# The first 400 tokens of a hybrid encoder block: loaded twice, or transposed on TensorE

## The chip, the cores and the metric

The kernel runs on one core of one Trainium2 chip. Its engines are TensorE (PE, whose weight loads the profile lists as PEld), VectorE (DVE), ScalarE (ACT), GpSimd (POOL) and SyncE (SP), whose queue issues all DMAs here. The metric is device time in microseconds (us) of one execution. The profile's times count from the first instruction of a profiled execution; "L810" is line 810 of the kernel before.

## What is computed

One layer of an encoder with two groups of heads. A sequence of 16 meta tokens, 256 prompt tokens and 2048 sample tokens (2320 in all, 1024 wide, float32) is normalised, projected to 2816 columns, handled by windowed attention and by a convolution, and projected back:

```python
def rmsnorm(x, w):
    y = x * lax.rsqrt(jnp.mean(x * x, axis=-1, keepdims=True) + NORM_EPS)
    return y * w

def hybrid_layer(z, norm_w, w_in, ..., w_out):
    h = rmsnorm(z, norm_w)
    proj = jnp.einsum('bld,de->ble', h, w_in)
    q, k, v, g_att, c_val, c_glu, g_conv = jnp.split(proj, SPLIT_IDX, axis=-1)
    ...
    att = windowed_gqa(q, k, v, sink) * jax.nn.silu(g_att)
    cnv = conformer_conv(c_val, c_glu, conv_w, conv_b, ln_w, ln_b) * jax.nn.silu(g_conv)
    mixed = jnp.concatenate([att, cnv], axis=-1)
    return z + jnp.einsum('ble,ed->bld', mixed, w_out)
```

The change touches only how `h` and the first weights reach TensorE at the start of the kernel.

## The kernel before

**Groups and units.** The tokens are cut into six groups: group 0 has 400 tokens (16 meta tokens and three blocks of 128), the others have 384. The columns of `w_in` are cut into units of 256. For the projections the tokens must lie along the free dimension and the 1024 inputs along the partitions, in eight steps `d` of 128. So the host passes `z` twice: by rows (`z`) and transposed (`zt`).

**Exact products.** A value is split into a high part (a cast to the fp32r type, by ScalarE) and a low part (the difference, by DVE or POOL). One exact product is three matmuls: high by high, high by low, low by high (`PASSES`). One sum of a projection (`proj_et`, L810) is 8 steps times 3, 24 matmuls into one bank of PSUM. A unit takes two sums for each group (its columns 0 to 127 and 128 to 255). The first items are unit 0 and unit 1 on group 0, then on group 1, then on group 2.

**Preparing a group.** `stats(i)` loads 128 rows of `z` (16 for i = 0) into a tile `xn`, squares them in place on ScalarE with a sum along the row (L679), and POOL makes `rstd` of the sum (L128, L129). `Prep.load` loads four pieces of `zt` of the group (L696); `first` lays `rstd` out along the free dimension by transposing its broadcast on TensorE (L708, into `bc`); `scale` multiplies `zt` by the norm weight and `bc` on DVE (L724); `split` makes high and low parts (L741 on ScalarE, L750 on DVE and POOL). Group g needs the stats 3g+1 to 3g+3, group 0 the stats 0 to 3.

**Weights.** `weights(k)` gives a load of four pieces (L776) and a split of each (L785 on ScalarE, L786 on DVE or POOL).

**Order.** Instructions are traced in program order and then arranged on each engine by a scheduler that simulates the engines' times. `tc.keep_in_program_order(op)` pins an instruction behind the one traced just before it on the same engine. It fixes the order only, and adds no wait for that one's result. An engine takes its instructions in this order, and waits at one whose inputs are not there.

**The opening (L1040 to L1063).** SP issues stats 0 to 3, `vecs` (norm weight and other small vectors), two pieces of `zt`, the four of unit 0, two more of `zt`, the convolution's weights. DVE derives `nsnk` and `kscale` from `vecs` (L1050, L1051). Then come the rests of stats 0 to 3, `first`, and piece by piece scaling, split of x and split of the weight. Stats 4 to 6 and the weights of unit 1 are loaded after that, and group 1's `zt` at the first item (`at_item_start`).

**Tiles.** Tag "us" (pool `cp`, four buffers) holds `xn` 0 to 5, then unit 1's raw weights, later the convolution's inputs. Tag "xn" (pool `sp`, two buffers) holds later `xn`. Tag "y" (pool `yp`, four buffers) holds the convolution's outputs. PSUM has four tags, "a" to "d", of two banks each; the sums use "a" and "b" in turn.

Of the kernel before, what the change touches and what calls it, by code (L numbers as in the profile page):

```python
# [11 lines left out]
F32 = mybir.dt.float32  # L12
F32R = mybir.dt.float32r
BF16 = mybir.dt.bfloat16
AF = mybir.ActivationFunctionType
ALU = mybir.AluOpType
AX = mybir.AxisListType

P = 128
D = 1024  # L20
ND = D // P
NM = 16
# [17 lines left out]
YW = 1280  # L40
UWID = 1197
# [23 lines left out]
GROUPS = [(0, 400)] + [(400 + 384 * i, 384) for i in range(5)]  # L65
# [14 lines left out]
def hymba_kernel(  # L80
# [11 lines left out]
    nc = tc.nc  # L92
# [3 lines left out]
    psum = ctx.enter_context(tc.tile_pool(name="psum", bufs=2, space=bass.MemoryType.PSUM))  # L96
# [11 lines left out]
    ident = const.tile([P, P], F32, name="ident")  # L108
    make_identity(nc, ident)
    vec = const.tile([P, 30], F32, name="vec")  # L110
    nw = vec[:, 0:8]
# [12 lines left out]
    rstd = const.tile([P, NB + 1], F32, name="rstd")  # L124
# [59 lines left out]
    yp = y_pools.enter_context(tc.tile_pool(name="yp", bufs=4, side="left"))  # L184
    wr = wr_pools.enter_context(tc.tile_pool(name="wr", bufs=1, side="right"))
    sp = right_pools.enter_context(tc.tile_pool(name="sp", bufs=2, side="right"))
    cp = right_pools.enter_context(tc.tile_pool(name="cp", bufs=4, side="right"))
# [475 lines left out]
        left_pools.close()  # L663

    if True:
        def stats(i):
            rows = NM if i == 0 else P
            r0 = 0 if i == 0 else NM + P * (i - 1)
            if i < 6:
                xn = cp.tile([P, UWID], F32, tag="us", name=f"xn{i}")[:, :D]  # L670
            else:
                xn = sp.tile([P, D], F32, tag="xn", name=f"xn{i}")
            dma = nc.sync.dma_start(xn[:rows], z[r0 : r0 + rows, :])
            if i >= PIN_X:
                tc.keep_in_program_order(dma)

            def rest():
                ssq = sp.tile([P, 1], F32, tag="ssq", name=f"ssq{i}", bufs=4)
                nc.scalar.activation(xn[:rows], xn[:rows], AF.Square, accum_out=ssq[:rows])  # L679
                rsqrt(rstd[:rows, i : i + 1], ssq[:rows], 1.0 / D, EPS)  # L680

            return rest

        xg = {}
# [70 lines left out]
        def weights(k):  # L755

            key = keys[k]
            raw = {}

            def load(eng):  # L760
                pool = wl if k % 2 else wr
                ws = pool.tile([P, ND, 2, UW], F32R, tag="ws", name=f"ws{key[0]}_{key[1]}")
                wsplit[key] = ws
                if key[0] == 1 and key[1] >= CACHE:
                    for q in range(4):
                        part = ws[:, 2 * q : 2 * q + 2].rearrange("p d a n -> p (d a n)")
                        eng.dma_start(part.bitcast(F32), wd[key[1], q])
                    return
                for q in range(4):
                    if k == 1:  # L770
                        if q % 2 == 0:
                            pair = cp.tile([P, UWID], F32, tag="us", name=f"wraw{k}_{q}")
                        raw[q] = pair[:, 512 * (q % 2) : 512 * (q % 2) + 512].rearrange("p (a n) -> p a n", n=UW)
                    else:
                        raw[q] = sp.tile([P, 2, UW], F32, tag="wraw", name=f"wraw{k}_{q}", bufs=4)
                    dma = eng.dma_start(raw[q], w_in[key[1], :, 2 * q : 2 * q + 2, :])  # L776
                    if PIN_W <= k < 4:
                        tc.keep_in_program_order(dma)

            def split(q, eng):  # L780
                if key[0] == 1 and key[1] >= CACHE:
                    return
                ws = wsplit[key]
                hi, lo = ws[:, 2 * q : 2 * q + 2, 0, :], ws[:, 2 * q : 2 * q + 2, 1, :]
                nc.scalar.copy(hi, raw[q])  # L785
                eng.tensor_tensor(lo, raw[q], hi, op=ALU.subtract)  # L786
                if key[0] == 0 and key[1] >= CACHE:
                    part = ws[:, 2 * q : 2 * q + 2].rearrange("p d a n -> p (d a n)")
                    later(1, lambda: nc.sync.dma_start(wd[key[1], q], part.bitcast(F32)))

            return load, split

        pj_n = [0]
# [42 lines left out]
        us = {}  # L836
# [200 lines left out]
        for k in range(2, len(keys)):  # L1037
            loads.setdefault(last_at[keys[k - 2]], []).append(k)

        preps = [Prep(g, False) for g in range(6)]  # L1040
        w01 = [weights(k) for k in range(2)]
        r = {i: stats(i) for i in (0, 1, 2, 3)}
        nc.sync.dma_start(vec[:, 0:28], vecs)
        preps[0].load(0)
        preps[0].load(1)
        w01[0][0](nc.sync)
        preps[0].load(2)
        preps[0].load(3)
        nc.sync.dma_start(cw, conv_w)
        nc.vector.tensor_scalar(nsnk, snk, -1.0, None, op0=ALU.mult)  # L1050
        nc.vector.scalar_tensor_tensor(kscale, vec[:, 20:21], -(HD ** -0.5), vec[:, 21:22], op0=ALU.mult, op1=ALU.mult)  # L1051
        for i in (0, 1, 2, 3):
            r[i]()
        preps[0].first()
        preps[0].alloc()
        preps[0].scale(0)
        for q in range(4):
            if q < 3:
                preps[0].scale(q + 1)
            preps[0].split(q)  # L1060
            w01[0][1](q, nc.gpsimd if q % 2 else nc.vector)
        r = {i: stats(i) for i in (4, 5, 6)}
        w01[1][0](nc.sync)  # L1063

        def at_item_start(i, c, u, g):
            if (c, u, g) == (1, ORDER[0], CHUNKS[1][1]):
                nc.sync.dma_start(km.bitcast(F32), kmd)
                for r0 in range(0, P, NM):
                    nc.sync.dma_start(vm[r0 : r0 + NM].rearrange("p a e -> p (a e)").bitcast(F32), vmd)
            if i == 0:  # L1070
                r[4]()
                r[5]()
                for q in range(4):
                    preps[1].load(q)
                    w01[1][1](q, nc.gpsimd if q % 2 else nc.vector)
                r[6]()
            if i == 1:
                later(1, preps[1].first)
                later(1, preps[1].alloc)
                later(1, lambda: preps[1].scale(0))  # L1080
                for q in range(4):
                    if q < 3:
                        later(1, lambda q=q: preps[1].scale(q + 1))
                    later(1, lambda q=q: preps[1].split(q))
                for k in range(7, 10):
                    later(1, lambda k=k: later(1, stats(k)))
                for q in range(4):
                    later(2, lambda q=q: preps[2].load(q))
            if i == I2:
                later(1, preps[2].first)  # L1090
                later(1, preps[2].alloc)
                later(1, lambda: preps[2].scale(0))
                for q in range(4):
                    if q < 3:
                        later(1, lambda q=q: preps[2].scale(q + 1))
                    later(1, lambda q=q: preps[2].split(q))
# [128 lines left out]
```

## Time and profile before

| | us |
|---|---|
| median of three runs | 963.74 (962.9 to 964.27) |
| the profiled execution's own time | 963.51 |
| its span, from first to last instruction | 961.7 |

In the profile each engine's busy time is given with its share of the span. A line of the timeline reads: start, duration of the group, engine, source line, operation, output tile <- input tiles, shapes, count; in brackets the idle time just before it and what ended it. A line of the view of waits reads: engine and tile that waited, what it waited for, then the total, the number and the longest. A line of a stage reads: the stretch and its length, then for PE, PEld, DVE, ACT and POOL the busy time and number of instructions, the granted TensorE clock (1.00 is full), the DMA share and GB/s. A line of a group of instructions reads: shapes and count, then busy time in us and mean of one in ns, then idle time before.

### The profile page before, as it was taken

The numbers are of one execution on the slowest core, as the hardware profiler recorded it, in microseconds if no ns is written. First come the engines' busy times: TensorE is split into PE (matmuls) and PEld (weight loads), VectorE is DVE, ScalarE is ACT, GpSimd is POOL, SyncE is SP. The second block draws the span as 40 slices with busy tenths as digits, with TensorE's granted clock in tenths as the row PEclk, the third lists the DMA queues.
The fourth block names the chain that finished last, engine by engine and source line by source line (L and its number), as shares of the span: only waits on it lengthen the run. The fifth ranks groups of instructions, "written<-read, shape, count | busy, mean of one in ns | idle before, by whom it ended". The sixth has DMA issues, their size and how long they took to land. (4 is left out here: it accounts for less than half of the span.)

```text
span 961.7 us, 16263 instructions
## 1 busy us (share of the span) xinstructions
PE 941.8 (98%) x5721; PEld 884.9 (92%) x5721; DVE 751.5 (78%) x1261; ACT 428.9 (45%) x1163; POOL 343.4 (36%) x542
## 2 busy tenths in 40 slices
PE   5999999999999999999999989999999999999998
PEld 4999999999999999999999989988888888888886
DVE  4659999988977789999996655767776777777773
ACT  7621112353458651011112456556665666656661
POOL 5600000264569300000002455655444554545442
PEclk9999999999999999999999999999999999999999
DMA  9653345784646597233334765964554355544411
GB/s 335 223 191 114 132 172 181 257 288 171 222 151 190 182 321 268 88 121 130 137 137 140 225 240 179 404 200 157 162 174 134 126 174 152 178 127 137 132 56 66
DMA packets 122528, 172.50 MB, mean 179 GB/s; under 512 B 10032, under 2 KB 84928, under 8 KB 122448
## 3 DMA queue, kind: packets, MB, share of 16 engines
q1 hardware_dynamic: 122448, 171.47, 52.7%
q8 instruction: 45, 0.74, 0.3%
q14 instruction: 35, 0.29, 0.1%
HBM read 108.74 MB, written 62.70 MB: 178 GB/s over the span
## 5 line engine op out<-in xcount | busy, mean ns | idle before, releaser
L810 PE MATMUL pj<-xh,ws 128*128 128x384 f32 (+1 forms) x1536 | 398.0, 340 | 2.8 <-ACT xh L741 2.8
L893 DVE SCALAR_TENSOR_TENSOR y<-us,cw,y 128x1167 f32<-128x1167 f32 x240 | 329.0, 1428 | 0.3
L810 PEld LDWEIGHTS pj<-xh,ws 128*128 128x128 f32 x1536 | 281.5, 189 | 3.1 <-ACT xh L741 3.1
L810 PE MATMUL pj<-xl,ws 128*128 128x384 f32 (+1 forms) x768 | 261.6, 341 | 0.0
L578 PE MATMUL y<-wo,rest 128*128 128x512 f32 x648 | 173.3, 404 | 0.0
L826 PE MATMUL pj<-ws,xh 128*128 128x256 f32 (+1 forms) x880 | 166.3, 285 | 1.4 <-DVE kn L982 1.0
L810 PEld LDWEIGHTS pj<-xl,ws 128*128 128x128 f32 x768 | 144.9, 189 | 0.4 <-DVE xl L750 0.3
L826 PEld LDWEIGHTS pj<-ws,xh 128*128 128x128 f32 (+1 forms) x880 | 137.5, 188 | 2.8 <-ACT sqq L927 1.2
L578 PEld LDWEIGHTS y<-wo,rest 128*128 128x128 f32 x648 | 115.2, 189 | 20.4
L826 PE MATMUL pj<-ws,xl 128*128 128x256 f32 (+1 forms) x440 | 124.8, 284 | 0.0
L416 ACT ACTIVATE sb<-sb,nm 128x304 f32<-128x304 f32 (+4 forms) x144 | 77.1, 535 | 61.9 <-DVE nm L404 59.3
L474 DVE TENSOR_TENSOR ptiles<-pT,ptiles 128x512 fp32r<-128x512 f32 x100 | 68.5, 686 | 31.4 <-ACT ptiles L473 30.7
L918 ACT ACTIVATE go<-pj 128x384 f32<-128x384 f32 x48 | 23.5, 490 | 153.5 <-PE pj L810 145.5
L404 DVE CUSTOM_DVE_ANT_0 sb<-S,bias,vec 128x304 f32<-128x304 f32 (+4 forms) x144 | 73.6, 511 | 14.6 <-PE S L349 11.8
L128 POOL TENSOR_SCALAR ssk<-ssk 128x2 f32<-128x2 f32 x18 | 9.3, 516 | 208.7 <-ACT sqk L932 206.8
L826 PEld LDWEIGHTS pj<-ws,xl 128*128 128x128 f32 (+1 forms) x440 | 83.0, 189 | 0.3
L439 POOL TENSOR_SCALAR sb<-sb,es 128x304 f32<-128x304 f32 (+4 forms) x144 | 71.9, 516 | 3.6
L473 ACT CAST ptiles<-pT 128x512 fp32r<-128x512 f32 x100 | 58.1, 581 | 32.0 <-PE pT L462 31.3
L497 PE MATMUL O<-ptiles,v 128*128 128x512 f32 x200 | 64.6, 402 | 0.0
L349 PEld LDWEIGHTS S<-kw,q 128*128 128x128 f32 x288 | 53.0, 188 | 12.6 <-issue 1.7
L349 PE MATMUL S<-kw,q 128*128 128x304 f32 (+4 forms) x288 | 61.9, 297 | 1.5 <-DVE q L372 1.5
L128 POOL TENSOR_SCALAR ssq<-ssq 128x4 f32<-128x4 f32 (+2 forms) x55 | 25.8, 470 | 101.7 <-ACT xn L679 78.0
(118 smaller groups left out, 1258.1 us busy)
## 6 DMA issues: line engine op xcount, KB each, us to landing
wd<-ws SPq DMA_DIRECT2D x36, 512.0 KB, 5.5
ws<-wd SPq DMA_DIRECT2D x36, 512.0 KB, 6.0
wraw<-in_w_in SPq DMA_DIRECT2D x52, 256.0 KB, 5.8
xn<-in_z SPq DMA_DIRECT2D x18, 512.0 KB, 5.9
gd<-go SPq DMA_DIRECT2D x48, 192.0 KB, 2.1
yo<-in_z SPq DMA_DIRECT2D x36, 256.0 KB, 3.4
out_y<-yo SPq DMA_DIRECT2D x36, 256.0 KB, 2.2
kw<-kd SPq DMA_DIRECT2D x16, 512.0 KB, 5.2
```

Of the source, the lines that this page charges most:

```text
L128: nc.gpsimd.tensor_scalar(src, src, scale, eps, op0=ALU.mult, op1=ALU.add)
L349: r = f(*a, **k)
L404: nc.vector.tensor_tensor_reduce(out=sb[:, n, c0:c1], in0=ps[:, 0:w], in1=cst["bias"][:, kv, n, c0 - QB * n : c1 - QB * n], scale=1.0, sca ...
L416: nc.scalar.activation(sb[:, n, c0:c1], sb[:, n, c0:c1], AF.Exp, bias=nm[:, n : n + 1], scale=-1.0, accum_out=rs[:, n : n + 1],)
L439: nc.gpsimd.tensor_scalar(sb[:, k, a0:a1], sb[:, k, a0:a1], es[:, k : k + 1], 1.0, op0=ALU.mult, op1=ALU.mult)
L473: nc.scalar.copy(ph, pt)
L474: nc.vector.tensor_tensor(pl, pt, ph, op=ALU.subtract)
L497: nc.tensor.matmul(o, lhs, t, start=(start and i == 0), stop=(stop and i == 1))
L578: nc.tensor.matmul(ps, mh[mi][:, e % 4, :], wo[e, wi][:, cols], start=(e == 4 and k == 0), stop=(e == 3 and k == 2),)
L810: nc.tensor.matmul(ps[:, :n], ws[:, d, wi, P * half_i : P * half_i + P], x[xi][:, d, o : o + n], start=(k == 0), stop=(k == 3 * ND - 1),)
L826: nc.tensor.matmul(ps[:rows, :UW], x[xi][:, d, o : o + rows], ws[:, d, wi, :], start=(k == 0), stop=(k == 3 * ND - 1),)
L893: nc.vector.scalar_tensor_tensor(y[:, yo + o0 : yo + o1], u[:, o0 + k : o1 + k], cw[:, j, k : k + 1], y[:, yo + o0 : yo + o1], op0=ALU.mul ...
```

## The change

For the first 400 tokens nothing is loaded from `zt`. `stats` 0 to 3 square into a tile of their own (`sq0`), so that the rows stay. DVE scales the rows by `rstd` in place. TensorE transposes them, 128 columns at a time (`turn0`), into eight PSUM tiles `cols0[d]`, which ScalarE and DVE turn into high and low part, multiplying with the norm weight as they read (`split0`). For `d` up to 5 the transposes are pinned in the order of the stats; those of `d` 6 and 7 follow when banks are free. Ahead of the transposes of each stat, TensorE multiplies the identity by itself: 20, 14, 4 and 5 times (`busy`), pinned in the same line. The opening's squares, row scalings and splits are pinned too. The weights of unit 1 are loaded directly behind those of unit 0, into "y" tiles, then stats 4 and 5, `zt` of group 1 and stat 6. `xn` 4 to 6 use the tag "xn". The low parts of unit 0 are all made by DVE.

```diff
+        rows0 = {}
+        sq0 = yp.tile([P, YW], F32, tag="y", name="sq0")
+        def pinned(op, yes=True):
+            if yes:
+                tc.keep_in_program_order(op)
...
-            if i < 6:
+            if i < 4:
                 xn = cp.tile([P, UWID], F32, tag="us", name=f"xn{i}")[:, :D]
+                rows0[i] = xn
             else:
                 xn = sp.tile([P, D], F32, tag="xn", name=f"xn{i}")
...
-                nc.scalar.activation(xn[:rows], xn[:rows], AF.Square, accum_out=ssq[:rows])
+                sq = sq0[:, :D] if i < 4 else xn
+                pinned(nc.scalar.activation(sq[:rows], xn[:rows], AF.Square, accum_out=ssq[:rows]), i < 7)
...
-                            pair = cp.tile([P, UWID], F32, tag="us", name=f"wraw{k}_{q}")
+                            pair = yp.tile([P, YW], F32, tag="y", name=f"wraw{k}_{q}")
...
-                nc.scalar.copy(hi, raw[q])
-                eng.tensor_tensor(lo, raw[q], hi, op=ALU.subtract)
+                pinned(nc.scalar.copy(hi, raw[q]), k < 2)
+                pinned(eng.tensor_tensor(lo, raw[q], hi, op=ALU.subtract), k < 2)
...
+        cols0 = {}
+        SEGS0 = [(0, NM), (NM, P), (NM + P, P), (NM + 2 * P, P)]
+        def busy(pt, n):
+            for _ in range(n):
+                tc.keep_in_program_order(nc.tensor.matmul(pt[:, :P], ident, ident, start=True, stop=True))
+        def turn0(i, d):
+            o, rows = SEGS0[i]
+            if d not in cols0:
+                cols0[d] = psum.tile([P, 512], F32, tag="cdcdabcd"[d], name=f"xt0_{d}")
+            return nc.tensor.transpose(
+                cols0[d][:, o : o + rows], rows0[i][:rows, P * d : P * d + P], ident[:rows, :rows]
+            )
+        def split0(d):
+            xh, xl = xg[0]
+            n = GROUPS[0][1]
+            pt = cols0[d]
+            pinned(nc.scalar.mul(xh[:, d, :n], pt[:, :n], nw[:, d : d + 1]))
+            pinned(
+                nc.vector.scalar_tensor_tensor(
+                    xl[:, d, :n], pt[:, :n], nw[:, d : d + 1], xh[:, d, :n], op0=ALU.mult, op1=ALU.subtract
+                )
+            )
...
-        preps[0].load(0)
-        preps[0].load(1)
         w01[0][0](nc.sync)
-        preps[0].load(2)
-        preps[0].load(3)
+        w01[1][0](nc.sync)
...
-        for i in (0, 1, 2, 3):
+        warmup = psum.tile([P, 512], F32, tag="a", name="warmup")
+        for i in range(4):
             r[i]()
-        preps[0].first()
+            o, rows = SEGS0[i]
+            pinned(nc.vector.tensor_scalar(rows0[i][:rows], rows0[i][:rows], rstd[:rows, i : i + 1], None, op0=ALU.mult))
+            busy(warmup, (20, 14, 4, 5)[i])
+            for d in range(6):
+                tc.keep_in_program_order(turn0(i, d))
         preps[0].alloc()
-        preps[0].scale(0)
+        r = {i: stats(i) for i in (4, 5)}
+        preps[1].load(0)
+        preps[1].load(1)
+        preps[1].load(2)
+        preps[1].load(3)
+        r[6] = stats(6)
         for q in range(4):
-            if q < 3:
-                preps[0].scale(q + 1)
-            preps[0].split(q)
-            w01[0][1](q, nc.gpsimd if q % 2 else nc.vector)
-        r = {i: stats(i) for i in (4, 5, 6)}
-        w01[1][0](nc.sync)
+            w01[0][1](q, nc.vector)
+            split0(2 * q)
+            split0(2 * q + 1)
+            if q in (0, 1):
+                for i in range(4):
+                    turn0(i, 6 + q)
...
                 for q in range(4):
-                    preps[1].load(q)
                     w01[1][1](q, nc.gpsimd if q % 2 else nc.vector)
```

## The prediction

> **What bounds the kernel now.** I read the page's busy table first, then the waits of TensorE (PE), then busy time by stage, then PE's timeline over the first 25 us.
>
> ```profile
> PE 941.8 (98%) x5721; PEld 884.9 (92%) x5721; DVE 751.5 (78%) x1261; ACT 428.9 (45%) x1163; POOL 343.4 (36%) x542
> ```
>
> ```profile
> PE bc L708 <- POOL rstd L129: 8.3, 4, 4.9
> PE pj L810 <- ACT xh L741: 2.8, 1, 2.8
> PE S L349 <- DVE q L372: 1.5, 1, 1.5
> ```
>
> ```profile
> 0.00:12.75 12.75, 1.71 (x4) 0.72 (x4) 2.99 (x8) 7.17 (x13) 3.68 (x14) 1.00 0.85 283
> 12.75:18.23 5.48, 5.48 (x16) 5.08 (x17) 4.85 (x8) 3.92 (x9) 5.02 (x4) 1.00 1.05 404
> 50.00:100.00 50.00, 50.00 (x283) 50.00 (x282) 40.24 (x44) 9.64 (x18) 2.91 (x3) 1.00 0.42 150
> 500.00:600.00 100.00, 96.21 (x759) 95.12 (x758) 61.79 (x124) 46.52 (x141) 41.99 (x102) 0.98 0.56 186
> 950.00:961.70 11.70, 7.93 (x35) 6.22 (x34) 1.72 (x3) 0.00 (x0) 0.00 (x0) 0.93 0.12 45
> ```
>
> PE is busy 98% of the span. Of its 19.9 us of idle time, 11.0 lie before 12.75 us (12.75 less 1.71 busy), 3.8 in 500 to 600 us and 3.8 in the tail. So whatever brings the projections forward in the first 25 us should come out at the end almost whole, and whatever delays them too. In the opening there is a second loss, which the busy time hides:
>
> ```profile
> 12.75 1.04 PE L810 MATMUL pj<-xh,ws 128*128 128x400 f32 x2 [2.78 <-ACT xh L741]
> 14.04 0.87 PE L810 MATMUL pj<-xh,ws 128*128 128x400 f32 x2
> 17.04 0.87 PE L810 MATMUL pj<-xh,ws 128*128 128x400 f32 x2
> 19.14 0.34 PE L810 MATMUL pj<-xh,ws 128*128 128x400 f32 x1
> 23.87 0.34 PE L810 MATMUL pj<-xh,ws 128*128 128x400 f32 x1
> 24.05 0.38 PE L708 MATMUL bc<-ident,rstd 128*128 128x128 f32 x2
> ```
>
> Between 14.04 and 17.04 nine products start, 0.333 us apart; from 19.14 to 23.87 it is 26, 0.182 us apart: a factor of 1.83, though the granted clock of both stretches reads 1.00. The slow pace holds for about 4.6 us after the first product at 12.75. Exactly 48 products (two sums of 24) start before 24.05. At 0.182 they would take 8.74 us; they take 11.30. PE therefore stands as if it had begun at full pace at 24.05 - 8.74 = **15.31 us**. That is the mark: the change gains what it gets below it, and loses what it adds above.
>
> **The change, part by part.** Four loads of zt (400 KB each), the eight scalings on DVE (L724), four broadcasts of rstd (L708) and POOL's share of the split go; x arrives through PE instead. The chain is then: rstd, scaling of rows on DVE, PE's queue, ScalarE's hi cast, first product.
>
> *Rows.* The scaling of the first rows is pinned behind the instruction traced just before it on DVE, which is kscale, and kscale waits for vecs.
>
> ```profile
> 1.00 0.29 POOL masks.py:199 TENSOR_SCALAR_AFFINE_SELECT ident<-ident 128x128 f32<-128x128 f32 x1
> 2.58 0.43 SPq L1043 DMA_DIRECT2D vec<-in_vecs  x1
> 7.72 0.17 DVE L1050 TENSOR_SCALAR vec<-vec 128x2 f32<-128x2 f32 x1 [6.86 <-DMA vec<-in_vecs]
> 7.79 0.15 DVE L1051 SCALAR_TENSOR_TENSOR kscale<-vec 128x1 f32<-128x1 f32 x1
> 8.90 0.55 POOL L129 TENSOR_TENSOR rstd<-ssq,half 128x1 f32<-128x1 f32 x1
> ```
>
> ```profile
> L884 DVE TENSOR_SCALAR y<-us,cw,vec 128x1167 f32<-128x1167 f32 x8 | 7.0, 881 | 0.0
> L853 ACT ACTIVATE sg<-pj 128x400 f32<-128x400 f32 x4 | 2.0, 500 | 3.1 <-PE pj L810 3.1
> L462 PE MATMUL pT<-ident,sb 128*128 128x128 f32 x400 | 60.0, 272 | 0.0
> ```
>
> vecs is issued behind the same rows of z as before, so kscale again ends at 7.94. A scaling of 1024 columns is not in the trace; L884's 0.88 us for 1167 bounds it from above, 0.77 in proportion from below; I take 0.81. First rows 8.75, then 9.56, 10.37, 11.18. The last rstd (8.90 + 0.55 = 9.45) comes earlier, so DVE sets these times.
>
> *PE's queue.* All of 43 identity products and 24 transposes are pinned in one line, 20 products before the first rows, then 14, 4 and 5. A transpose costs about 0.088: four of L462 fill the time from 640.61 to 640.96.
>
> ```profile
> 640.61 0.60 PE L462 MATMUL pT<-ident,sb 128*128 128x128 f32 x4
> 640.96 1.63 PE L578 MATMUL y<-wo,rest 128*128 128x512 f32 x6
> ```
>
> A plain product of two f32 operands is not in the trace: its projections work on operands that were cast to fp32r, three products for one exact one. The low end is the transpose, 0.088; the high end L462's own duration, 0.27, if nothing overlapped. The nearest row is the exact product in three: 3 x 0.182 x 128/400 = 0.17 by L810's pace, 3 x 0.088 = 0.26 by L462's. I take the middle, 0.22 warm and 1.83 times that, 0.40, in the first 4.6 us.
>
> The Trainium skill ("FP8 and Floating Point Precision", TensorE Precision Notes) says that true FP32 makes four passes through the array; with "TensorE: Matmul & The Clock Gate" (53 ns for 128 columns) an estimate of 0.21 follows, and the sum below would be 0.2 us smaller. No run here shows it.
>
> Sum: start at 1.29 with the identity; 4.6 us at 0.40 are 11.5 products; the other 8.5 take 1.87, to 7.8; wait for rows to 8.75. Then 6 x 0.088 + 14 x 0.22 = 3.61, to 12.36; 0.53 + 0.88, to 13.77; 0.53 + 1.10, to 15.40; the first transpose of the last rows is out 0.27 later, 15.67, long after the rows (11.18). ScalarE's cast out of PSUM takes L853's 0.50: **first product at 16.2 us**, warm. The weights are no bar (ACT had them at 11.66 before, and they now follow z directly in the queue).
>
> *Feed after that.* Both sums of the unit use the same d, so each pair of d gives PE 12 x 0.182 = 2.18 us of work.
>
> ```profile
> 10.02 2.25 DVE L724 SCALAR_TENSOR_TENSOR xt<-xt,vec,bc 128x400 f32<-128x400 f32 x4 [2.07 <-PE bc L708]
> 11.66 0.62 ACT L785 CAST ws<-wraw 128x512 fp32r<-128x512 f32 x1 [3.12 <-DMA wraw<-in_w_in]
> 12.31 0.69 DVE L786 TENSOR_TENSOR ws<-wraw,ws 128x512 fp32r<-128x512 f32 x1
> ```
>
> DVE needs 0.69 + 2 x 0.56 (L724 also reads one operand from PSUM) = 1.81 for it, ACT 0.62 + 2 x 0.50 = 1.62: both hidden under PE, as long as the two sums alternate. If PE did only one sum at a time, DVE would set 1.81 against 1.09 and up to 2.9 us would show; I price that at nothing since before ran the pair without a gap. Eight more transposes, of d 6 and 7, fall among the products: 0.70. Squaring into a tile of its own, and weights in y tiles, cost nothing: same instructions, other addresses; those tiles have no other user before the convolution (59.7 us). The earlier issue of w1 and group 1's zt meets no PE wait, so brings nothing.
>
> So 48 products end at 16.2 + 8.74 + 0.70 = 25.64 against 24.05: **1.6 us later**. The sum goes on the profiled execution's own 963.51 (span 961.7 and 1.8 around it): **965.1 us**, or 0.16% slower; the median of the runs shown, 963.74, is 0.2 higher than that execution. The order of later work is planned anew; the waits from 200 to 600 us (5.1 us) bound that, and I allow 1 us either way.
>
> **The rivals.** A measurement of this kernel can tell about 0.2%, 1.9 us, from no change; I use that bound for all chances.
>
> *Slower: the identity products cost more.* Behind the rows' arrival stand 23 products, so 0.01 us on each is 0.23 us at the end; from 0.234 on the kernel is over 0.2% slower. At the high end, 0.27, the 20 end at 8.7 (0.48 while slow), and 0.53 + 3.78 + 0.53 + 1.08 + 0.53 + 1.35 from 8.75 lead to a first product at 17.3: +2.7, 966.2. For it: nothing in the trace shows such a product cheap. Against: L810 shows 400 columns streaming in 0.182. Chance 0.20.
>
> *Faster: PE is never behind the rows.* If the scheduler had kscale's wait out of the way, rows would be ready at 4.88 + 0.81 = 5.7 up to 9.45 + 0.81 = 10.26, and with products cheap enough (43 of them and 24 transposes in 8.97 us, 0.16 each over the cold stretch too) the first product would come at 10.26 + 0.27 + 0.50 = 11.0, warm: 48 done at 20.5, -3.5 us, 960.0; with the vecs wait kept 11.95 and -2.7, 960.8. Against: the pin behind kscale, and 14 products between two rows only 0.81 apart. Chance 0.20, since both prices rest on rows I had to infer.
>
> *No change: products at 0.088.* The 20 end at 4.5 even at the slow pace (0.16), and PE idles until 8.75. If it stays warm, the first product comes at 13.1, -1.5; if it has fallen back, 6 + 14 + 6 + 4 + 6 + 5 at 0.16, then 0.088 from 13.35, put it at 15.3, +0.7. Result 962.0 to 964.2; 0.10. Which of the two is what the Trainium skill's rule decides ("TensorE: Matmul & The Clock Gate", Part 1): idle beyond a window of 3.4 us throttles the array again. Here the gap would be 4.2 us; before idled 2.78 us just ahead of 12.75 with four lone transposes behind it and was slow, which agrees but does not test the length.
>
> *Slower: group 1 late.* xn6 now shares two buffers with xn4, so its load waits for xn4's Square, and that is pinned behind all of ACT's casts.
>
> ```profile
> 9.92 2.83 SPq L673 DMA_DIRECT2D xn<-in_z  x3
> 36.00 1.06 ACT L679 ACTIVATE xn<-xn 128x1024 f32<-128x1024 f32 x1 [2.00 <-DMA xn<-in_z]
> xn<-in_z SPq DMA_DIRECT2D x18, 512.0 KB, 5.9
> ```
>
> Casts end at 15.67 + 4 x 1.62 = 22.2, Square 4 at 23.4; load 5.9, to 29.3; Square, rstd, broadcast, scaling and cast (1.25 + 0.75 + 0.3 + 0.56 + 0.52) to 32.7. Group 1's first product is due at 25.64 + 8.74 = 34.4. It costs only from a landing time of 7.6 us on; at 10 us, with sigmoids held behind the pinned Square, +2 to +4 on my sum: 967 to 969. Before shows such a wait on ACT (2.00 us at 36.0). Chance 0.12.
>
> **How the numbers follow.** Forecast (965.1, own range 964.0 to 965.6) 0.38; dearer products 0.20; rows in time 0.20; cheap products 0.10; group 1 late 0.12. Faster 0.20, within the bound 0.38 + 0.10 = 0.48, slower 0.32. The range drops the outer half of the fastest case and of the slowest: 961.0 to 967.8.
>
> **What would show it.** In the profile after: the mean interval of the identity products (0.22 warm, 0.40 in the first 4 to 5 us); DVE's first row scaling at 7.9, the last ending at 11.2; PE's first projection at 16.2 and from there 0.182 apart; the 48th done at 25.6; no L679 wait that PE shows at 34. A first projection before 14.2 proves the price too high, after 16.6 too low. A gap between the first 24 and the next 24 products would show that the sums do not alternate.

## The result, and the profile after it

| | before | after |
|---|---|---|
| median | 963.63 us (962.9 to 964.27) | 970.26 us (969.82 to 971.32) |
| profiled execution | 963.51 (span 961.7) | 969.82 (span 967.7) |

The ratio is 1.0063, 95% interval 1.0048 to 1.0078: slower by 0.6%. The forecast of 965.1 had the sign, but the time lies above its range (961.0 to 967.8). In the profiled pair 6.3 us are to be found; the sum of the prediction had 1.6.

First the page's busy row of the kernel after, then the rows of its waits on TensorE (engine and tile that waited, for what, total, number, longest).

```profile
PE 954.8 (99%) x5835; PEld 898.3 (93%) x5835; DVE 751.8 (78%) x1263; ACT 428.4 (44%) x1163; POOL 339.3 (35%) x536
```

```profile
PE pj L819 <- DVE xl L759: 1.8, 1, 1.8
PE pj L835 <- DVE qs L964: 1.7, 2, 1.3
PE warmup L1055 <- POOL ident masks.py:199: 1.3, 1, 1.3
```

PE's busy time rose by 13.0 us (954.8 less 941.8) and the span by 6.0. The opening's idle time is indeed gone: of the 11 us before the first product 1.3 are left. But it is filled with work that the end does not need, so that a higher busy share says nothing here. Two waits are new: 1.8 us at the projections of group 1 and 1.3 of the 1.7 us before q's columns.

Where the 6 us arise is read off instructions that both traces have: the end of the same instruction in one and in the other. Three of them, a gate of the convolution near 124 us, a later one near 515, and an addition to the output near 635, in the timeline of before:

```profile
123.15 0.49 ACT L918 ACTIVATE go<-pj 128x384 f32<-128x384 f32 x1 [0.74 <-PE pj L810]
...
514.86 0.49 ACT L918 ACTIVATE go<-pj 128x384 f32<-128x384 f32 x1 [3.75 <-PE pj L810]
...
634.32 0.69 DVE L589 TENSOR_TENSOR yo<-y,yo 128x512 f32<-128x512 f32 x1 [0.61 <-PE y L578]
```

and in that of after:

```profile
127.88 0.49 ACT L927 ACTIVATE go<-pj 128x384 f32<-128x384 f32 x1 [0.75 <-PE pj L819]
...
519.59 0.49 ACT L927 ACTIVATE go<-pj 128x384 f32<-128x384 f32 x1 [3.75 <-PE pj L819]
...
640.46 0.69 DVE L589 TENSOR_TENSOR yo<-y,yo 128x512 f32<-128x512 f32 x1 [0.61 <-PE y L578]
```

The lag is 4.7 us at 124, 4.7 at 515 and 6.1 at 635; the last addition, near 959, has 6.1 as well (the tables below give it from unrounded times). So two places cost: the first 50 us, and 550 to 635. All runs below are compared by this lag behind the profiled run of before (below zero: ahead of it).

**The opening.** PE's timeline of the kernel after:

```profile
1.34 7.27 PE L1055 MATMUL warmup<-ident 128*128 128x128 f32 x40 [1.34 <-POOL ident masks.py:199]
8.55 0.54 PE L1062 MATMUL xt<-ident,xn 16*128 16x16 f32 x6
9.02 3.39 PE L1055 MATMUL warmup<-ident 128*128 128x128 f32 x28
12.25 0.82 PE L1062 MATMUL xt<-ident,xn 128*128 128x128 f32 x6
12.90 1.06 PE L1055 MATMUL warmup<-ident 128*128 128x128 f32 x8
13.79 0.82 PE L1062 MATMUL xt<-ident,xn 128*128 128x128 f32 x6
14.45 1.28 PE L1055 MATMUL warmup<-ident 128*128 128x128 f32 x10
15.57 0.82 PE L1062 MATMUL xt<-ident,xn 128*128 128x128 f32 x6
16.52 0.63 PE L819 MATMUL pj<-xh,ws 128*128 128x400 f32 x2
17.19 0.71 PE L1062 MATMUL xt<-ident,xn 16*128 16x16 f32 x4
17.66 0.43 PE L819 MATMUL pj<-xl,ws 128*128 128x400 f32 x1
...
26.75 0.27 PE L717 MATMUL bc<-ident,rstd 128*128 128x128 f32 x1
```

Each identity product leaves two records: x40 are the 20, x28 the 14. Five of them fill the time from 14.45 to 15.57, 0.224 us each: the price of the forecast was 0.22. The first projection comes at 16.52 (forecast 16.2), and behind the first few the products are 0.182 apart. The first transposes of the last rows come at 15.57, though those rows are ready at 11.42 (10.67 + 0.75, below): PE stands behind its own identity products, not behind data.

**Group 1.** The same timeline further on, rows of ScalarE, POOL, PE and DVE:

```profile
23.35 2.22 ACT L794 CAST ws<-wraw 128x512 fp32r<-128x512 f32 x4
26.15 1.06 ACT L688 ACTIVATE xn<-xn 128x1024 f32<-128x1024 f32 x1 [0.59 <-DMA xn<-in_z]
...
27.96 0.55 POOL L129 TENSOR_TENSOR rstd<-ssq,half 128x1 f32<-128x1 f32 x1
...
32.80 0.27 PE L717 MATMUL bc<-ident,rstd 128*128 128x128 f32 x1
...
33.11 4.29 DVE L733 SCALAR_TENSOR_TENSOR xt<-xt,vec,bc 128x384 f32<-128x384 f32 x8 [3.24 <-PE bc L717]
...
38.68 0.44 PE L819 MATMUL pj<-xl,ws 128*128 128x384 f32 x1 [1.84 <-DVE xl L759]
```

Read backwards: PE waits 1.84 us for a low part of group 1, since DVE began the eight scalings only at 33.11, after 3.24 us without work, waiting for the third broadcast of `rstd` on PE. That broadcast is not late for lack of its input: rstd 6 is ready at 28.51 (27.96 + 0.55), and PE takes the broadcast at 32.80, 4.3 us later, because it stands behind group 0's products in PE's order. My theory is that rstd 6 is late in the plan because Square 6 is pinned on ScalarE behind the four casts of unit 1's weights (23.35 to 25.57). The wait on the load that the prediction feared is the 0.59 in brackets.

**Late.** The other 1.4 us, 550 to 635, are taken up with the third set of experiments.

### The profile page after: what moved, and what is told of

Same layout as the page of the kernel before. It is cut to its first block, busy times and chain, and to the rows that moved or that the text cites. A ratio compares the mean times of both kernels' runs of the same rounds, so it can differ in the third digit from the quotient of the medians.

```text
span 967.7 us, 16481 instructions
## 1 busy us (share of the span) xinstructions
PE 954.8 (99%) x5835; PEld 898.3 (93%) x5835; DVE 751.8 (78%) x1263; ACT 428.4 (44%) x1163; POOL 339.3 (35%) x536
```

## The experiments

Of the tables' columns, "first" is the start of the first projection, "48th" that of the 48th product (before: 12.75 and 23.87), and the lag at 124, 515 and 635 us is worked out as above. The times are medians; the kernel before had 964.2 to 964.4 beside these runs, and 963.63 beside the kernel after. A lag speaks of the one profiled execution, and that can lie below the median of its kernel: 965.22 against 967.34 in `e3_none`, 961.78 against 963.21 in `before_warm`.

### First set: is it the load, or PE's identity products?

Two theories for group 1: the load of stat 6, which shares two buffers with stat 4, comes too late; or the order, Square 6 behind the casts of unit 1. And for the opening: the identity products cost what they take, or they are needed for the pace.

`e1_xn6_own` gives the stat its own tile, so that its load waits for nothing:

```diff
-            else:
+            elif i == 6:
+                xn = yp.tile([P, YW], F32, tag="y", name=f"xn{i}")[:, :D]
+            else:
```

> Stat 6 gets a buffer of its own (a y tile), so its load no longer waits for stat 4's square. Theory (the 6 us are 2.9 us of late start, 1.84 us of group 1 coming late through stat 6, and 1.4 us met after 500 us): the load of xn6 is issued before 14 us, its rstd is there before 27 us, PE's wait of 1.84 us for xl at 36.8 us is gone, the first projection stays at 16.5 us, and the time falls by 1.8 us, to about 968.3 (0.5% over before). Rival (group 1 is late because PE and the splits are late altogether, not because of stat 6): the wait stays over 1 us and the time within 0.5 us of 970.3.

`e2_few` changes the counts of identity products as below, `e3_none` has none, `e4_few_xn6` is `e2_few` with the tile of its own:

```diff
-            busy(warmup, (20, 14, 4, 5)[i])
+            busy(warmup, (20, 0, 0, 3)[i])
```

> Identity products 20, 0, 0, 3 instead of 20, 14, 4, 5. Theory (the products behind the first rows hold the transposes back, 0.224 us each): the rows of stat 3 are scaled at 11.4 us, the first projection starts at 12.3 to 12.6 us at full pace (0.182 us apart), 4 us earlier than with 43 products, and the time falls by 2.2 to 4 us, to 966.3 to 968, with the wait for group 1 growing where stat 6 stays late. Rival (the clock needs those products; with fewer, PE falls back to the slow pace): the first projections run 0.33 us apart for about 4 us and at most 2 us are gained.

> No identity products at all. If they only buy the clock: first projection at 12.1 to 12.5 us, then about 4.6 us at 0.33 us apart, so 2 us worse than with the 20, 0, 0, 3 and still about 2 us better than with 43. If transposes alone bring the clock up: as good as 20, 0, 0, 3.

> Both: products 20, 0, 0, 3 and a buffer of its own for stat 6. If the two losses are separate they add: 4 us and 1.8 us, 964 to 964.6, level with before within 0.2%. If the second one only shows when PE starts late, it gives no more than the few products alone gave.

| run | first | 48th | lag at 124 | 515 | 635 | time | ratio (95%) |
|---|---|---|---|---|---|---|---|
| after | 16.52 | 26.56 | 4.74 | 4.73 | 6.14 | 970.26 | 1.0063 (1.0048 to 1.0078) |
| e1_xn6_own | 16.68 | 26.72 | 4.64 | 4.60 | 5.44 | 969.56 | 1.0060 (1.0045 to 1.0075) |
| e2_few | 12.56 | 22.61 | 0.82 | 0.79 | 2.54 | 966.25 | 1.0026 (1.0015 to 1.0038) |
| e3_none | 12.96 | 23.00 | 0.40 | 0.38 | 1.78 | 967.34 | 1.0029 (1.0017 to 1.0042) |
| e4_few_xn6 | 12.54 | 22.59 | 0.35 | 0.32 | 2.41 | 966.21 | 1.0023 (1.0013 to 1.0032) |

The load is not it: with the tile of its own the lag at 124 stays within 0.1, and PE's wait falls only from 1.84 to 1.59 us. In `e1_xn6_own` Square 6 follows the casts without a wait, at 25.58. POOL then has low parts of unit 1 until 27.78, so rstd 6 is there at 28.68, and the broadcast still comes at 32.95:

```profile
28.13 0.55 POOL L129 TENSOR_TENSOR rstd<-ssq,half 128x1 f32<-128x1 f32 x1
...
32.95 0.27 PE L719 MATMUL bc<-ident,rstd 128*128 128x128 f32 x1
```

Most of the identity products are a price without a return. Without the 14, the 4 and two of the 5 the first projection comes 3.96 us earlier. Without any it comes at 12.96, and PE is at full pace there too; so the 23 that `e2_few` keeps bring 0.40 us. By the medians `e3_none` is 1.1 us slower than `e2_few`, though its profiled execution is the faster one. PE's timeline of `e3_none`:

```profile
8.50 4.58 PE L1062 MATMUL xt<-ident,xn 16*128 16x16 f32 x24 [8.50 <-DVE xn L1090]
12.96 0.64 PE L819 MATMUL pj<-xh,ws 128*128 128x400 f32 x2
```

From its first projection to its 48th product it needs 10.04 us, exactly what the kernel after needs (26.56 less 16.52). The 24 transposes, 0.19 us each on average, take the slow time on themselves: most come 0.213 us apart, the last two, from 12.7 us on, 0.11. The Trainium skill ("TensorE: Matmul & The Clock Gate", Part 4) holds that in transposes the full clock doesn't engage; here 4.46 us of nothing but transposes are followed by products at full pace, so the measurement decides against it.

Yet with the 48th product 1.26 us ahead of before, `e2_few` is 0.82 behind at 124 us: group 1 and group 2 take back 2.1. And 0.8 to 2.1 more are lost behind 515, in all of these kernels.

### Second set: the order, the pace alone, and vecs

`r6_early` is `e1_xn6_own` with the rest of stat 6 traced ahead of the casts of unit 1; `few_r6` is the same with the counts of `e2_few`:

```diff
                 r[5]()
+                r[6]()
                 for q in range(4):
                     w01[1][1](q, nc.gpsimd if q % 2 else nc.vector)
-                r[6]()
```

> The kernel after with xn6 in a tile of its own and the rest of stat 6 (Square 6 and rstd 6) traced ahead of the four splits of unit 1's weights, so that ScalarE takes Square 6 before the four w1 casts. Theory (group 1 is late because the pin puts Square 6 behind those casts, and with it the third broadcast of rstd behind group 0's products in TensorE's order): the third broadcast leaves 32.8 us for about 27 to 29, DVE's scaling of group 1 begins before 31 instead of 33.1, the gap of 1.84 us before 38.7 falls under 0.4, the lag at 50 us behind the kernel before falls from 4.7 to about 2.9. The loss of 1.4 us between 550 and 632 stays, since q's casts are still placed early in ScalarE's order. Time 967.8 to 968.6, ratio about 1.0045. Rival (group 1 waits for its loads or for POOL): the gap stays over 1.2 us, the time 969.5 or more.

> The same, with 20, 0, 0 and 3 identity products. ScalarE's order around the q casts of the first softmax is here that of the kernel before. Theory (the loss between 550 and 632 us comes with that order): first projection about 12.55, 48th product about 22.8, the gap before q at 597 is 0.4 instead of 1.1 to 1.3, and the lag grows by 0.9 or less after 550 us instead of 2.05 in the same opening without the move (0.35 to 2.40). A gap of about 1 us at 32 us, where the broadcast of group 2 waits for POOL's rstd, may stay. Time 964.3 to 965.2, ratio 1.000 to 1.001. Rival (the late loss comes with any earlier opening, by the clock): 966.0 to 966.5, ratio 1.0023, with a gap of 1 us or more before q at 597.

`nogate` has that too, with 12, 4, 2 and 2 identity products, and the two instructions that wait for `vecs` behind the row scalings:

```diff
-        nc.vector.tensor_scalar(nsnk, snk, -1.0, None, op0=ALU.mult)
-        nc.vector.scalar_tensor_tensor(kscale, vec[:, 20:21], -(HD ** -0.5), vec[:, 21:22], op0=ALU.mult, op1=ALU.mult)
...
             for d in range(6):
                 tc.keep_in_program_order(turn0(i, d))
+        pinned(nc.vector.tensor_scalar(nsnk, snk, -1.0, None, op0=ALU.mult))
+        pinned(nc.vector.scalar_tensor_tensor(kscale, vec[:, 20:21], -(HD ** -0.5), vec[:, 21:22], op0=ALU.mult, op1=ALU.mult))
```

> As before with xn6 of its own and Square 6 early, and nsnk and kscale, which wait for vecs, traced behind the four row scalings, so that vecs no longer holds these; 12, 4, 2 and 2 identity products. Theory (rows are held by vecs; without that the last rows' rstd, 9.5 to 10.7, sets the start): first row scaling at about 5.5 instead of 7.7, last ending at 10.5 to 11.4, first projection 11.7 to 12.5 at the full pace of 0.182, 48th product 21.9 to 22.8 against 24.05 in the kernel before. With a lag of -1.5 to -2.1 there, about 1 us given back by group 2's broadcast at 32 us and 0.5 late, 962.5 to 964.0, ratio 0.9985 to 1.000. Rival (the array needs the identity products): a pace of 0.33 for the first products, 48th product after 24, 965 or more.

`before_warm` is the kernel before with identity products, and with the four broadcasts of `rstd` pinned in one line with them; x is loaded transposed as ever:

```diff
-                    nc.tensor.transpose(
+                    op = nc.tensor.transpose(
...
+                    if g == 0:
+                        tc.keep_in_program_order(op)
...
+        busy(20)
         preps[0].first()
+        busy(12)
         preps[0].alloc()
```

> The kernel before, with 20 identity products ahead of and 12 behind the four broadcasts of rstd, and nothing else: the pace alone. Theory (the slow 4.6 us behind the first product come from PE's idling before it, not from its operands): first projection at 12.75 as before, products 0.182 apart from the start, 48th product starts at about 22.0 to 22.4 instead of 23.87, lag -1.6 to -2.0 from there to 500 us. The q casts stand early in ScalarE's order here, so up to 1.4 is lost late: 962.0 to 963.8, ratio 0.998 to 1.000. Rival (the feed of group 0, not the pace, sets the first 48): products no closer than 0.25 apart, 48th product after 23.5, time within 0.3 of the kernel before or above it.

| run | first | 48th | lag at 124 | 515 | 635 | time | ratio (95%) |
|---|---|---|---|---|---|---|---|
| r6_early | 16.52 | 26.57 | 2.66 | 2.16 | 2.42 | 965.58 | 1.0018 (1.0009 to 1.0027) |
| few_r6 | 12.62 | 22.67 | 0.96 | 0.45 | 1.76 | 966.10 | 1.0018 (1.0009 to 1.0027) |
| nogate | 12.27 | 22.31 | 2.41 | 1.93 | 2.61 | 966.37 | 1.0023 (1.0014 to 1.0032) |
| before_warm | 12.46 | 23.36 | -0.70 | -1.58 | -2.04 | 963.21 | 0.9986 (0.9977 to 0.9995) |

`r6_early` settles group 1. Its opening is that of the kernel after to 0.01 us (48th product), and its lag at 124 us is 2.66 instead of 4.64. Its timeline:

```profile
23.50 1.06 ACT L690 ACTIVATE xn<-xn 128x1024 f32<-128x1024 f32 x1
...
24.55 2.17 ACT L796 CAST ws<-wraw 128x512 fp32r<-128x512 f32 x4
...
25.01 0.55 POOL L129 TENSOR_TENSOR rstd<-ssq,half 128x1 f32<-128x1 f32 x1
...
27.71 0.27 PE L719 MATMUL bc<-ident,rstd 128*128 128x128 f32 x1
...
28.02 4.29 DVE L735 SCALAR_TENSOR_TENSOR xt<-xt,vec,bc 128x384 f32<-128x384 f32 x8 [0.42 <-PE bc L719]
```

The third broadcast is at 27.71, not 32.95, and PE has no wait at group 1. The edit moves stat 6 on both engines, ahead of the casts on ScalarE and of the low parts on POOL; which of the two counts was not tested apart. The time came out over 2 us below what I had expected: the late loss is only 0.26 here, where I had 1.4, and 0.5 more was gained between 124 and 515 us, where PE idles 0.5 us less than in before.

The same move in a shorter opening fails. In `few_r6` and `nogate` the square is now ahead of the casts, its data are not there yet, and PE waits for the casts, 1.97 us in the one and 2.40 in the other. PE's row of `few_r6`, then that of `nogate`:

```profile
25.20 0.45 PE L821 MATMUL pj<-xh,ws 128*128 128x400 f32 x1 [1.97 <-ACT ws L796]
```

```profile
25.28 0.70 PE L821 MATMUL pj<-xh,ws 128*128 128x400 f32 x1 [2.40 <-ACT ws L796]
```

In `nogate` it costs more than its length, since the granted clock reads 0.50 from 24.89 to 28.30 behind it; behind the wait in `few_r6` it stays at 1.00. Both times are misses, by 0.9 and 2.4 us, for a reason that I had not asked about: a fixed order behind a load that the shorter opening now overtakes. Of the late loss, `few_r6` has 1.31 instead of the 2.09 of `e4_few_xn6`, with a gap of 0.45 us before q's columns instead of 1.35. That is a miss too (0.9 or less was expected), though q's casts stand where the kernel before has them; the third set shows what the rest is. `nogate` also shows that `vecs` is not worth moving: its first projection is 0.3 us earlier than that of `few_r6`, as the last rows are scaled at 11.20 instead of 11.55 (each of them waits for POOL's `rstd`).

`before_warm` gains 2.0 us of span in the profiled pair (1.7 of the execution's own time), and is faster than before by 0.14% (0.05 to 0.23%). So part of the slow stretch that the prediction read in the kernel before can be had without transposing anything. But only 0.7 us of the gain lie in the opening; 0.9 come between 124 and 515 us and 0.5 behind that, where the code is the same; 0.5 and 0.3 of them are idle time of PE that is gone. Of the 1.6 to 2.0 that I expected in the opening most of the rest went to a wait behind POOL, which has the low part of a weight ahead of that of x (timeline, POOL and PE):

```profile
12.99 1.57 POOL L788 TENSOR_TENSOR ws<-wraw,ws 128x512 fp32r<-128x512 f32 x1 [3.34 <-ACT ws L787]
14.52 2.81 POOL L752 TENSOR_TENSOR xl<-xt,xh 128x400 fp32r<-128x400 f32 x2
...
16.05 0.45 PE L812 MATMUL pj<-xl,ws 128*128 128x400 f32 x1 [1.22 <-POOL xl L752]
```

### Third set: the late loss, and a kernel with both repairs

In the kernel after, the order of ScalarE near 592 us differs from before in one thing that counts: the two casts that split q of block 1 (L369, L370) stand ahead of the table load of the layer norm's `zn`, not behind that norm. The timeline of after, ScalarE and DVE:

```profile
591.44 0.57 ACT L369 CAST q<-qT 64x512 fp32r<-64x512 f32 x1
592.02 0.58 ACT L370 CAST q<-qT 64x512 fp32r<-64x512 f32 x1
592.62 1.28 ACT L223 ACT_TABLE_LOAD   x1
...
597.63 0.63 ACT L936 ACTIVATE sqq<-pj 128x256 f32<-128x256 f32 x2
...
598.02 0.42 DVE L937 TENSOR_REDUCE ssq<-sqq 128x4 f32<-128x256 f32 x1 [3.52 <-ACT sqq L936]
```

By the 1.15 us of these casts all that follows is late: the squares of the next columns of q at 597.63, DVE's sum that waited 3.52 us for them, and PE, which stands 1.31 us at the next columns because DVE has not yet taken earlier ones out of PSUM. `q_pin` is the kernel after with that order put back by one pin:

```diff
-        later(1, lambda: q_split(pt, q2))
+        later(1, lambda: q_split(pt, q2, b))
...
-        nc.scalar.copy(dst[0][0:64], src[0:64])
+        pin(b == 1)(nc.scalar.copy)(dst[0][0:64], src[0:64])
```

> The kernel after with one more pin: the first of the two casts that split q of block 1 (line 369) is pinned behind the square traced just before it on ScalarE. By that these casts stand in ScalarE's order where they stand in the kernel before, behind the zn of the layer norm and two squares, and not ahead of the table load of that zn. Theory (1 us of the 1.4 that are lost between 550 and 632 us comes from that place): the gap before q's columns near 597 us falls from 1.31 to 0.45 or less, the lag at 632 us from 6.1 to 5.2 to 5.5, the time to 968.9 to 969.5, ratio about 1.0052. Rival (few us shift, any order does it): the gap stays at 1 us or more and the time at 970.0 or above.

`few_l6` is `few_r6` with stat 6 loaded together with 4 and 5, ahead of group 1's `zt`, and `few_l6_q` has the pin as well:

```diff
-        r = {i: stats(i) for i in (4, 5)}
+        r = {i: stats(i) for i in (4, 5, 6)}
...
-        r[6] = stats(6)
```

> 20, 0, 0 and 3 identity products, xn6 in a tile of its own, Square 6 ahead of unit 1's casts on ScalarE, and now stat 6 loaded together with stats 4 and 5, ahead of group 1's zt. Theory (in the same kernel with the later load ScalarE waited 3.9 us for that load with unit 1's casts behind it, which cost TensorE 1.97 us at 23): that gap is gone, the 48th product starts at about 22.8, TensorE shows no gap over 0.3 between 13 and 50 us, the lag behind the kernel before is -0.8 to -1.2 at 50 us. q's casts stand early in ScalarE's order, so 1.0 to 2.0 is lost late: 963.5 to 965.0, ratio 0.9995 to 1.001. Rival (transposing gains nothing in the opening): lag at 50 us above -0.3.

> The run with the earlier load of stat 6 and the pin of q's casts together. Theory: the same opening, the gap before q's columns near 595 us at 0.45 or less, 0.5 to 1.0 us faster than without the pin: 962.8 to 964.0, ratio 0.9985 to 1.000. Rival (the place of q's casts is not the cause): no more than 0.3 us between the two.

`warm_dve` is `before_warm` with all low parts of unit 0's weights made by DVE:

```diff
-            w01[0][1](q, nc.gpsimd if q % 2 else nc.vector)
+            w01[0][1](q, nc.vector)
```

> The kernel before with 20 and 12 identity products around the broadcasts, and the low parts of unit 0's weights all made by DVE, as the change does, so that POOL's low parts of x are not queued behind them (that queue cost TensorE 1.22 us at 14.8 in the run with the products alone). Theory: no gap over 0.4 between 12.5 and 24 us, 48th product at about 22.3 to 22.8 instead of 23.4, lag -1.5 to -2.0 at 50 us and -2.5 to -3.0 at the end: 962.0 to 962.8, ratio 0.998. Rival (DVE, with 2.4 us of work for each pair of d against TensorE's 2.2, now sets the pace): gaps of 0.2 to 0.5 at each pair, 48th product after 23.4, 963.2 or more.

| run | first | 48th | lag at 124 | 515 | 635 | time | ratio (95%) |
|---|---|---|---|---|---|---|---|
| q_pin | 17.00 | 27.03 | 4.45 | 4.40 | 5.54 | 969.22 | 1.0047 (1.0034 to 1.0059) |
| few_l6 | 12.59 | 22.63 | -1.28 | -1.83 | -0.82 | 963.09 | 0.9985 (0.9976 to 0.9994) |
| few_l6_q | 12.63 | 22.67 | -1.25 | -2.25 | -2.15 | 962.19 | 0.9981 (0.9972 to 0.9990) |
| warm_dve | 12.56 | 24.10 | 0.03 | -1.00 | 2.73 | 965.92 | 1.0019 (1.0010 to 1.0028) |

The clean pair is `few_l6` and `few_l6_q`: from 515 to 635 us the one loses 1.01 us, the other 0.10. The view of waits, first of `few_l6`, then of `few_l6_q`:

```profile
PE pj L837 <- DVE qs L966: 2.0, 2, 1.4
```

```profile
PE pj L837 <- DVE qs L966: 0.5, 2, 0.3
```

The medians are 0.9 us apart. So the place of q's casts costs about 1 us, and it is reached by nothing that the change edits: the scheduler had planned the whole program anew behind a changed opening. In `q_pin` the gap falls from 1.31 to 0.24 and the time lies where it was expected, but the lag grows by 1.1 still. That is the granted clock. Near 570 us PE idles three times within 5 us in every kernel, and behind that the clock reads 0.50 for a while, with 1.00 just ahead of it and behind it. These stretches (start and end, length, busy time of PE, PEld, DVE, ACT, POOL with instructions, granted clock, DMA share, GB/s) of before, then after, then `q_pin`:

```profile
574.42:577.83 3.41, 3.41 (x18) 3.41 (x18) 1.71 (x5) 1.64 (x3) 2.21 (x5) 0.50 0.32 115
```

```profile
576.73:583.56 6.83, 5.68 (x25) 5.34 (x26) 4.09 (x9) 3.32 (x7) 2.71 (x6) 0.50 0.28 103
```

```profile
577.66:584.49 6.83, 5.48 (x26) 5.51 (x27) 3.24 (x8) 3.20 (x7) 2.21 (x5) 0.50 0.23 80
```

The low stretch lasts 3.41 us in the one and twice that in the others. Of the 14 profiled executions eight have 3.41 there, and six 6.83 (after, `e2_few`, `e4_few_xn6`, `few_r6`, `q_pin`, `warm_dve`). With it the late loss, from 515 to 635 us, can be split. PE's busy time between the two instructions of the lag (115.82 of 119.66 us in before, 116.70 of 121.08 in after) gives what PE idled more than in before, and by how much its own work took longer:

| run | late loss | more idle time | work longer by | clock at 0.50 |
|---|---|---|---|---|
| after | 1.41 | 0.54 | 0.88 | 6.83 |
| few_r6 | 1.31 | 0.43 | 0.88 | 6.83 |
| q_pin | 1.14 | 0.12 | 1.02 | 6.83 |
| r6_early | 0.26 | 0.07 | 0.18 | 3.41 |
| few_l6 | 1.01 | 1.13 | -0.13 | 3.41 |
| few_l6_q | 0.10 | 0.07 | 0.03 | 3.41 |

So the place of the casts acts by idle time, and the pair of `few_l6` and `few_l6_q` is clean in the clock too. The other part, 0.9 to 1.0 us in the first three rows, comes with a low stretch of double length. That is not the change alone, for executions of one and the same kernel have both: of 79 of the kernel before that ran beside the experiments, 53 have a mean granted clock of 0.997 or 0.998 and take 963.9 us on average, 26 have 0.996 and take 965.1. All four executions of the kernel after have 0.996, and 970.4 on average. At an equal clock the change costs some 5.3 us (an estimate, from these two means of separate sets of runs), and the pin of `q_pin`, which has 969.1 in its four executions at 0.996, gains 1.3. What makes the stretch single or double stays open; no run here was made for it.

`few_l6` and `few_l6_q` beat both kernels; they lie 0.4 and 0.6 us below the ranges that I had expected. In the opening they do what the change could do: 48th product 1.2 us earlier than before, no wait of PE at groups 1 and 2. Whether transposing is worth anything beside the pace is not settled: `before_warm`, without a transposed x, has 0.9986 (0.9977 to 0.9995), and the intervals overlap. `warm_dve` is a miss. Taking the weights from POOL did not free PE; DVE became the bound of the opening as its rival said (in PE's timeline waits of 0.21, 0.51, 0.16 and 0.81 us, 48th product at 24.10), and 3.7 us more went in 515 to 635: 1.4 of it idle time of PE and 2.3 longer work, more than the double low stretch costs elsewhere; that was not followed.

## Why the prediction was wrong, step by step

- **The mark, 15.31 us as if at full pace: right.** `before_warm` ran at full pace from its first product, with x fed as before, and got ahead. The slow pace behind it was read too short: products of the kernel before come 0.333 us apart up to 18.04, for 5.3 us and not 4.6. The mark does not use that length.
- **Rows: right where it counts.** DVE's scalings begin at 7.72, behind kscale as forecast, at 0.74 us each (2.23 for three) and not 0.81. The last one ends at 11.42, for another reason than the forecast's 11.18: it waited for POOL. The timeline of after:

```profile
7.72 2.23 DVE L1090 TENSOR_SCALAR xn<-xn,rstd 16x1024 f32<-16x1024 f32 x3
10.67 0.75 DVE L1090 TENSOR_SCALAR xn<-xn,rstd 128x1024 f32<-128x1024 f32 x1 [0.72 <-POOL rstd L129]
...
7.65 1.51 POOL L129 TENSOR_TENSOR rstd<-ssq,half 128x1 f32<-128x1 f32 x1
```

- **Price of an identity product: right, 0.224 against 0.22.** The estimate of 0.21 that the prediction worked out from the Trainium skill ("FP8 and Floating Point Precision", TensorE Precision Notes) is nearly as close. The slow stretch was longer: the 20 took 7.21 us (1.34 to 8.55). Their records, two for each, come 0.213 us apart up to 6.7 us and 0.112 behind that, so 5.4 us went at 0.43 a product, where 4.6 at 0.40 had been taken. In `q_pin` the same 20 took 6.09, 2.9 us of it slow, so this varies (its first projection is later all the same, since `vecs` came 0.5 us later and with it the rows). It cost almost nothing, as the first rows are ready only at 8.46, and the transposes begin at 8.55 where the forecast had 8.75.
- **First projection: 16.52 instead of 16.2, by small sizes.** The three sets of six transposes ahead of the last rows took 1.78 instead of 1.59 (0.109 for one of 128 rows, not 0.088), the 23 products 5.24 instead of 5.06, and from the last rows' first transpose to the first projection it was 0.95 instead of 0.8; the earlier start gave 0.2 back. The rival of dearer products (0.27) fell, and so did that of cheap ones. What rule of idle time would bring the slow pace back was not tested.
- **Feed: a term sized too small.** 48 products take 10.23 us (16.52 to 26.75), forecast 9.44. Two sets of four transposes take 0.47 each, 0.94, where 0.70 had been set; some 0.5 lie in longer intervals of the first products and beside the transposes (0.27 to 0.38 instead of 0.18). The sums did alternate: the 24th product starts at 22.21, ahead of the last low part, which DVE ends at 22.74. Opening in all: 2.7 us late, forecast 1.6.
- **Group 1: the step that failed.** The sum put "the earlier issue of w1 and group 1's zt meets no PE wait, so brings nothing", and its lateness was a rival with a chance of 0.12, by way of stat 6's load. It cost 2.0 us (4.74 less 2.7), by another way: stat 6 ordered behind unit 1's weights, on ScalarE by the pin and on POOL behind the low parts, and through the plan a broadcast on PE 4.3 us behind its input. The rival's price, 2 to 4 us, was met at its lower end, but that is luck: its mechanism was refuted by `e1_xn6_own`, while `r6_early`, which differs from that run in the order alone, took the 2.0 us away.
- **Planning of later work: allowed 1 us either way, it cost 1.4.** The place of q's casts costs about 1.0 (1.31 us of idle time instead of 0.35 before q's columns; `few_l6` against `few_l6_q`), of which a shorter wait at 579 gives 0.5 back. The other 0.9 go with the low clock behind 570 us, which lasted twice as long in this profiled execution; the prediction had no term for it.
- **"Faster, if rows came in time": the rival had the wrong lever.** Not the rows but the count of identity products decided: with 23 instead of 43 the opening gains 4 us against the change. I had asked what each of them costs and not whether they are needed.

So 6.1 us at the end are 1.6 as forecast, 1.1 by sizes in the opening, 2.0 at group 1, 1.4 late.

## What to carry to other kernels

Work that is put in to keep an engine's pace should be counted out against the pace that real work behind it brings anyway: here the needed transposes alone brought it but for 0.4 us, and 20 of the 43 products cost 4 us. When an order is pinned, ask of each pinned instruction what stands behind it on its engine and who waits for that, in this stage and the next; the same move gained 2.0 us at 124 us in a long opening and cost 0.6 in a short one (`few_r6` against `e4_few_xn6`), with a new wait of 2.0. And where a scheduler plans the whole program, a change at 10 us can cost 1 us at 595: compare the order of the instructions on each engine there, ahead of looking for a cause in the change. Compare the granted clock of the two executions as well: here one more low stretch was worth as much as the order.

## What the runs showed of the hardware

- PE is slow for the first 2.9 to 5.4 us of its steady work, whatever the work: projections in the kernel before (5.3 us), identity products (5.4 us in the kernel after, 2.9 in `q_pin`), transposes alone in `e3_none` (4.2 us). The Trainium skill ("TensorE: Matmul & The Clock Gate", Part 1) says that the length of this start varies from run to run; the 20 products of the same opening, 7.21 us in the kernel after and 6.09 in `q_pin`, agree.
- The granted clock reads 1.00 in this slow start only because the trace's record of it begins where the full pace does (18.05 us in the kernel before, 6.71 in the kernel after, 4.23 in `q_pin`, 12.68 in `e3_none`).
- Idle times of 2.4 us and less can be followed by a low clock: 0.50 for 3.41 or 6.83 us near 575, where PE idles for 1.16, 0.72 and 1.0 to 1.5 us within 5 us, and for 3.41 us behind the wait of 2.40 us in `nogate`. The wait of 1.97 us in `few_r6` and 1.59 us behind the 20 products in `q_pin` were followed by none.
- POOL's last step of `rstd`, on a column of 128, took 1.51 us in the kernel after while DVE was scaling rows of 1024 beside it, and 0.55 to 0.58 in the others of the first 60 us. Why was not tested.
